# Taking all four output pieces of a feed-forward block ahead of its weight forms

## The chip, the cores and the metric

The kernel runs on one core of a Trainium2 chip. The metric is the device time of one execution in microseconds; lower is better. Its engines are named as in the profile: PE (TensorE, matrix products), DVE (VectorE), ACT (ScalarE), POOL (GpSimd) and SP (SyncE, which here issues the weight loads).

## The reference

One decoder layer on 256 tokens of width 2048, all in 32-bit floats. Two feed-forward layers stand around a token mixer (sparse attention and a gated recurrence); after each of the three a layer norm. Only the feed-forward layers matter here:

```python
def swiglu(h, w_in, w_out):
    a, b = jnp.split(h @ w_in, 2, axis=-1)
    return (jax.nn.silu(a) * b) @ w_out
...
h = layer_norm(DN_ALPHA * h + 0.5 * swiglu(h, ffn1_w_in[l], ffn1_w_out[l]), ln1_g[l], ln1_b[l])
```

`w_in` is 2048 x 11264 and `w_out` 5632 x 2048, so each layer reads 138 MB of weights.

## The kernel before

**Precision.** Every 32-bit weight and activation is split in a high half (ACT copies it to a rounded type) and a low half (DVE subtracts the high half from the original). A product takes three matmuls: high by high, high by low, low by high (`three`, lines 743 to 745).

**Blocks.** A feed-forward layer has 22 blocks (n = 0 to 21) of 256 hidden columns, `blockF` with `gate` behind it. A block's first product, tokens by `w_in`, is summed over 16 slices of 128 rows. It is done in four chunks of four slices, and in blocks 6 to 21 all four chunks use a Strassen-like scheme with 7 products of half size where 8 are usual. A chunk then has four *forms*, pieces of weights: `p1q3`, `p2`, `q5p7` and `q4p6`, with 12, 6, 12 and 12 matmuls of 256 columns. The sixteen forms of a block are called F1 to F16 here: F1 to F4 are chunk 0, F5 to F8 chunk 1, and so on; F6 is `p2` of chunk 1, F15 is `q5p7` of chunk 3. DVE makes the sums and differences of weights that a form needs (`ws` L230 for `p1q3`, L234 for `p2`, L237 for `q5p7`), then ACT (L275) and DVE (L276) split it. There is one `ws` buffer.

**Output pieces.** The second product, gate by `w_out`, is interleaved with the first as *output pieces* (`"o"` in a plan). The layer's blocks lie in segments (0-1, 2-5, 6-9, 10-13, 14-17, 18-21). While a segment's blocks are computed, the output pieces of the segment before are multiplied: four in each of the blocks 6 to 21, called O1 to O4, each 12 matmuls of 512 columns. The four add up one product of 512 output columns, which ACT then empties (`yd`, L1174) and POOL adds to a sum in memory. O1 and O3 are split like forms (`raw` L275, L276). O2 and O4 are *far* pieces: loaded and split early, with two ACT copies for each half (L182, L185) and a POOL transfer that adds the weights to the negated high half in place of DVE's subtraction.

**Order.** PE, SP and POOL run in the order in which the code emits their work. ACT and DVE are ordered by a planner when the kernel is built, which takes what is ready and, among that, what was emitted earlier. Everything is emitted piece by piece by `Weights.unit`:

```python
            self.far_to(self.cur + EARLY)
            self.load_to(self.cur + AHEAD + LOADS)
            self.split_to(self.limit or min(self.cur + AHEAD, self.cap))
            self.on_piece(self.size(self.cur) * (1 if self.pieces[self.cur][1] else 2))
```

with `EARLY = 12`, `AHEAD = 4`, `LOADS = 4`. Split weights of all pieces but the far ones go to `hl` tiles, of which there are five (`HL_BUFS`): a piece can be split when the piece five before it (far ones not counted) has been multiplied.

**Gate.** When a block's forms are done, DVE and ACT put the seven products together to `z` and multiply its two halves (L1132 to L1145). That task then lets `LAG_T[0]` pieces of the next block begin, and with the last of them, ahead of its matmuls, emits four transposes on PE (T, L1151, reading `z`, of which there is one) and the split of their result: ACT L878, DVE L879, ACT L878, DVE L879, tile `g`. With a lag of 7 T stands ahead of the block's seventh piece, which is F4 in blocks 6 to 21.

**Plans.** `block_plan(chunks, fills, lead)` puts `lead` output pieces first, then the forms, and spreads the other `fills - lead` among these. In blocks 6 to 21, with 4 fills and a lead of 3: O1 O2 O3 F1 to F8 O4 F9 to F16.

Of the kernel before, what the change touches and what calls it, by code (L numbers as in the profile page):

```python
# [22 lines left out]
SEGS = ((0, 2), (2, 6), (6, 10), (10, 14), (14, 18), (18, 22))  # L23
# [44 lines left out]
FAST = (0, 1, 2, 3)  # L68
# [4 lines left out]
def block_plan(chunks, fills, lead=2, n=4, late=True):  # L73

    plain = [("c", k) for q in range(n) if q not in chunks for k in (4 * q, 4 * q + 2)]
    forms = [(f, q) for q in chunks for f in FORMS]
    rest = ["o"] * fills
    plan = [(rest.pop(), 0) for _ in range(min(lead, fills))] + plain[:1]  # L80
    plain = plain[1:]
    slow = []
    while plain or rest:
        for which in (plain, rest) if late else (rest, plain):
            if which:
                p = which.pop(0)
                slow.append((p, 0) if p == "o" else p)
    if not forms:
        return plan + slow
    step = len(forms) / (len(slow) + 1)  # L90
    n = 0
    for i, f in enumerate(forms):
        plan.append(f)
        while len(slow) > n and i + 1 >= (n + 1) * step:
            plan.append(slow[n])
            n += 1
    return plan


FOUR = tuple(range(6, 22))  # L100


def layer_plans():
    three = (1, 2, 3)
    plans = [block_plan((), 0)] * 2
    plans += [block_plan((1, 3), 2, 0)] + [block_plan(three, 2, 2, late=False)] * 3
    for n in range(6, NBK):
        plans.append(block_plan(FAST if n in FOUR else three, 4, 3))
    return plans


FILLS = [(g, nb, 2 * p) for g, (b0, b1) in enumerate(SEGS[:-1]) for nb in range(4) for p in range(b1 - b0)]
PLANS = layer_plans()
FAST_MORE = (2, 3, 1)
AWAY = (0, 1, 4, 7, 10, 13)
# [13 lines left out]
OUT_LAST = ([(nb, k) for nb in (0, 1) for k in (0, 2, 4)] + [(nb, 6) for nb in (0, 1)]  # L129
            + [(nb, k) for nb in (2, 3) for k in (0, 2, 4, 6)])  # L130

LAG_T = (7, 6)
LAG_LN = 4
WIDE = 2
LAG_ROPE = 6
# [232 lines left out]
def tile_layer(ctx, tc, x_fm, x_tm, pos, f1a, f1o, wA, wki, wB, wG, lru, wab, wrb, wo, f2a, f2o,  # L368
# [755 lines left out]
    def ffn(x, forms, ln):  # L1124
        def gate(c, e, g, i, lag, plain):

            z = W.fast_pool.tile([P, 4 * S], F32, name=name("z"), tag="z", bufs=Z_BUFS)
            z4 = z.rearrange("p (j c) -> p j c", j=4)
            a, b = z4[:, 0:4:2], z4[:, 1:4:2]
            if e:  # L1130
                p1, p6, p7, q5 = e[0][:, :S], e[0][:, S:], e[1][:, :S], e[1][:, S:]
                A.activation(z4[:, 0], p1, AF.Copy)  # L1132
                V.tensor_tensor(z4[:, 1], z4[:, 0], p6, op=OP.add)
                V.tensor_tensor(z4[:, 2], z4[:, 1], p7, op=OP.add)
                V.tensor_tensor(b, q5[:, None, :].to_broadcast([P, 2, S]), z4[:, 1:3], op=OP.subtract)
                for t in range(2):
                    w = 512 if plain or t == 0 else S
                    zt = z[:, t * 512:t * 512 + w]
                    V.tensor_tensor(zt, zt, c[t][:, :w], op=OP.add)  # L1139
                A.activation(a, a, AF.Silu)  # L1140
            else:
                for t in range(2):
                    A.activation(z4[:, 2 * t], c[t][:, :S], AF.Silu)
                    A.activation(z4[:, 2 * t + 1], c[t][:, S:], AF.Copy)
            V.tensor_tensor(a, a, b, op=OP.mult)  # L1145
            for _ in range(lag):
                yield
            ps = BP()
            for k in range(2):
                for t in range(2):  # L1150
                    T.transpose(ps[:, k * S + t * P:k * S + (t + 1) * P], z[:, t * 512 + k * P:t * 512 + (k + 1) * P], ident)  # L1151
            with tc.high_priority() if lag == LAG_T[1] else nullcontext():
                for k in range(2):
                    hl = UHL("g")
                    split(hl, ps[:, k * S:(k + 1) * S])
                    g[i + k] = hl
# [20 lines left out]
        for s, (b0, b1) in enumerate(SEGS):  # L1177
            for n in range(b0, b1):
                c, e = blockF(x, forms, PLANS[n], fill)
                task = gate(c, e, g[s], 2 * (n - b0), LAG_T[n == NBK - 1], ("c", 0) in PLANS[n])  # L1180
                with tc.high_priority():
# [514 lines left out]
```

## Time and profile before

| | us |
|---|---|
| three runs | 2337.8, 2341.34, 2342.86 |
| median | 2341.34 |
| profiled execution | 2340.27 |
| its span, first to last instruction | 2338.4 |
| PE busy in the span | 2312.5 |
| DVE busy in the span | 2201.5 |
| ACT busy in the span | 1560.0 |

The profile is of one execution. Busy is the time in which an engine had an instruction of its own running; matmuls are pipelined and overlap, and their ends are modelled, so their starts are the better guide. An instruction that starts before the end of the one ahead of it on its engine is not an error of the table: it is how closely they follow each other.

### The profile page before, as it was taken

How to read it: one execution, taken by the hardware profiler on the slowest of the kernel's cores; microseconds unless marked ns; L12 is line 12 of the kernel's file. 1: busy time of each engine (PE TensorE's matmuls, PEld its weight loads, DVE VectorE, ACT ScalarE, POOL GpSimd, SP SyncE). 2: the span in 40 equal slices, each digit the busy share in tenths (PEclk: the TensorE clock that was granted, in tenths of full speed). 3: DMA queues.
4: the chain of work that ended last, by engine and by line, in shares of the span. 5: the costliest groups of instructions: out<-in, count | busy, mean ns of one | idle time of the engine just before them, and what ended most of it. 6: DMA issues, size and time to landing. Idle time of an engine off the chain costs nothing.

```text
span 2338.4 us, 40427 instructions
## 1 busy us (share of the span) xinstructions
PE 2312.5 (99%) x15430; PEld 2109.4 (90%) x15430; DVE 2201.5 (94%) x3196; ACT 1560.0 (67%) x2273; POOL 263.4 (11%) x368
## 2 busy tenths in 40 slices
PE   9999999999999999999999999999999999999998
PEld 7899999999988999888899998888889999999997
DVE  7999999999999999979887888998999999999997
ACT  7667777777757656556557785555667777777763
POOL 1101111111110000000100001100111111111111
PEclk9999999999999999999999999999999999999999
DMA  9878988888876556554675658655788888888875
GB/s 336 251 238 240 261 250 251 250 256 250 230 244 209 192 187 216 185 189 154 244 239 193 200 182 326 239 198 195 242 275 232 253 255 252 243 252 267 244 221 215
DMA packets 142178, 546.97 MB, mean 234 GB/s; under 512 B 16640, under 2 KB 17280, under 8 KB 117536
## 3 DMA queue, kind: packets, MB, share of 16 engines
q1 hardware_dynamic: 100800, 455.00, 55.1%
q0 software_dynamic: 41040, 89.27, 18.4%
q8 instruction: 120, 1.97, 0.3%
q14 instruction: 74, 0.61, 0.1%
q10 hardware_dynamic: 144, 0.13, 0.0%
HBM read 507.10 MB, written 37.22 MB: 233 GB/s over the span
## 4 chain that ended last, share of the span: by engine, by line
PE 66%; DVE 23%; issue 5%; DMA 3%; ACT 2%; POOL 0%; SPq 0%; ACTq 0%; DVEq 0%; POOLq 0%
PE mm L743 13%; PE mm L745 13%; PE mm L744 13%; DVE hl L276 13%; PE bp L744 5%; PE bp L745 5%; PE bp L743 4%; PE mm L1390 3%; PE mm L1389 3%; PE mm L1391 3%; DVE ws L230 2%; DVE rf L237 2%; DVE rf L234 2%; ACT hl L275 2%; DMA raw<-f1o 1%
## 5 line engine op out<-in xcount | busy, mean ns | idle before, releaser
L275 ACT ACTIVATE hl<-rf 128x1024 fp32r<-128x1024 f32 x573 | 511.3, 912 | 232.9 <-DVE rf L237 119.7
L276 DVE TENSOR_TENSOR hl<-rf,hl 128x1024 fp32r<-128x1024 f32 x573 | 596.9, 1047 | 8.2 <-ACT hl L275 3.8
L276 DVE TENSOR_TENSOR hl<-raw,hl 128x1024 fp32r<-128x1024 f32 (+3 forms) x402 | 474.2, 1196 | 62.2 <-ACT hl L275 61.4
L275 ACT ACTIVATE hl<-raw 128x1024 fp32r<-128x1024 f32 (+3 forms) x402 | 408.4, 1035 | 179.4 <-PE mm L745 82.8
L744 PE MATMUL bp<-hl,sh 128*128 128x256 f32 x1146 | 323.6, 282 | 10.1 <-DVE hl L276 10.1
L743 PE MATMUL bp<-hl,sh 128*128 128x256 f32 x1146 | 320.9, 280 | 0.0
L745 PE MATMUL bp<-hl,sl 128*128 128x256 f32 x1146 | 320.2, 279 | 0.0
L743 PE MATMUL mm<-hl,hs 128*128 128x512 f32 (+1 forms) x800 | 274.5, 343 | 1.6 <-DVE z L1139 0.7
L275 ACT ACTIVATE hl<-ws 128x1024 fp32r<-128x1024 f32 x191 | 202.0, 1058 | 102.7 <-DVE ws L230 71.5
L744 PE MATMUL mm<-hl,hs 128*128 128x512 f32 (+1 forms) x800 | 268.3, 335 | 0.0
L745 PE MATMUL mm<-hl,hs 128*128 128x512 f32 (+1 forms) x800 | 267.9, 335 | 0.1
L230 DVE TENSOR_TENSOR ws<-rf 128x1024 f32<-128x1024 f32 x191 | 233.8, 1224 | 5.4 <-DMA rf<-wrb 1.3
L276 DVE TENSOR_TENSOR hl<-ws,hl 128x1024 fp32r<-128x1024 f32 x191 | 234.2, 1226 | 1.8 <-ACT hl L275 1.7
L744 PEld LDWEIGHTS bp<-hl,sh 128*128 128x128 f32 x1146 | 215.4, 188 | 17.5 <-DVE hl L276 16.3
L745 PEld LDWEIGHTS bp<-hl,sl 128*128 128x128 f32 x1146 | 217.7, 190 | 0.0
L743 PEld LDWEIGHTS bp<-hl,sh 128*128 128x128 f32 x1146 | 215.4, 188 | 1.3
L1389 PE MATMUL mm<-hs,hl 128*128 128x256 f32 x640 | 178.3, 279 | 0.0
L1391 PE MATMUL mm<-hs,hl 128*128 128x256 f32 x640 | 177.8, 278 | 0.0
L1390 PE MATMUL mm<-hs,hl 128*128 128x256 f32 x640 | 177.7, 278 | 0.0
L743 PEld LDWEIGHTS mm<-hl,hs 128*128 128x128 f32 x800 | 150.4, 188 | 19.1 <-issue 2.6
L745 PEld LDWEIGHTS mm<-hl,hs 128*128 128x128 f32 x800 | 151.0, 189 | 16.7 <-DVE hs L937 0.5
L744 PEld LDWEIGHTS mm<-hl,hs 128*128 128x128 f32 x800 | 150.5, 188 | 14.3 <-DVE hl L276 0.2
(360 smaller groups left out, 5897.6 us busy)
## 6 DMA issues: line engine op xcount, KB each, us to landing
rf<-f1a SPq DMA_DIRECT2D x75, 1024.0 KB, 7.7
rf<-f2a SPq DMA_DIRECT2D x75, 1024.0 KB, 7.5
raw<-f1o SPq DMA_DIRECT2D x88, 512.0 KB, 6.6
raw<-f2o SPq DMA_DIRECT2D x88, 512.0 KB, 6.6
raw<-wB SPq DMA_DIRECT2D x80, 512.0 KB, 4.8
raw<-wG SPq DMA_DIRECT2D x54, 512.0 KB, 4.2
ya<-yd POOLq DMA_DIRECT2D x80, 256.0 KB, 7.4
rf<-wA SPq DMA_DIRECT2D x20, 1024.0 KB, 5.5
```

The source lines that it names most:

```text
L230: v.tensor_tensor(t, b[:, 0:4:3], b[:, 1:2].to_broadcast([P, 2, 2, 256]), op=OP.add)
L234: v.tensor_tensor(b[:, 1], t[:, 1], b[:, 0], op=OP.add)
L237: v.tensor_tensor(b[:, 0], b[:, 1], b[:, 2], op=OP.add)
L275: nc.scalar.activation(hp, src, AF.Copy)
L276: self.last = nc.vector.tensor_tensor(lp, src, hp, op=OP.subtract)
L743: T.matmul(ps, xh, w[0], start=start, stop=False)
L744: T.matmul(ps, xh, w[1], start=False, stop=False)
L745: T.matmul(ps, xl, w[0], start=False, stop=stop)
L1389: T.matmul(ps[:, :S], w[0], x[:, 0], start=first, stop=False)
L1390: T.matmul(ps[:, :S], w[0], x[:, 1], start=False, stop=False)
L1391: T.matmul(ps[:, :S], w[1], x[:, 0], start=False, stop=last)
```

## The change

Blocks that are not the first of a segment get a lead of 4: O1 O2 O3 O4 F1 to F16. The first blocks of the segments (6, 10, 14, 18) keep their plan, since their O4 multiplies the gate of the block just before. The lag of the transposes goes from 7 pieces to 5, for all blocks but the last of a layer. T then stands ahead of a block's fifth piece: between O4 and F1 in the blocks with the new plan, between F1 and F2 in blocks 6, 10, 14 and 18.

```diff
     for n in range(6, NBK):
-        plans.append(block_plan(FAST if n in FOUR else three, 4, 3))
+        plans.append(block_plan(FAST if n in FOUR else three, 4, 3 if any(n == b for b, _ in SEGS) else 4))
     return plans
...
-LAG_T = (7, 6)
+LAG_T = (5, 6)
```

## Rows read from the trace of the kernel before

**Rows 1.** The page, part 1: busy us, share of the span, instructions.
```profile
PE 2312.5 (99%) x15430; PEld 2109.4 (90%) x15430; DVE 2201.5 (94%) x3196; ACT 1560.0 (67%) x2273; POOL 263.4 (11%) x368
```
**Rows 2.** Windows, blocks 6-21 of each layer: length, busy us, clock, DMA share, GB/s.
```profile
159.30:661.61 502.31, 497.64 (x3522) 464.44 (x3521) 500.04 (x608) 361.08 (x504) 85.97 (x100) 1.00 0.85 247
1781.32:2283.43 502.11, 497.32 (x3522) 463.81 (x3521) 500.37 (x609) 360.57 (x503) 85.72 (x100) 1.00 0.83 247
```
**Rows 3.** PE's waits, whole span: total us, times, longest.
```profile
PE bp L744 <- DVE hl L276: 10.1, 30, 0.6
```
**Rows 4.** Timeline of DVE, one block: start us, us, instruction, count.
```profile
471.32 2.35 DVE L276 TENSOR_TENSOR hl<-raw,hl 128x1024 fp32r<-128x1024 f32 x2
...
480.99 0.69 DVE L1145 TENSOR_TENSOR z<-z 128x512 f32<-128x512 f32 x1
...
482.73 1.22 DVE L230 TENSOR_TENSOR ws<-rf 128x1024 f32<-128x1024 f32 x1
...
485.60 0.69 DVE L276 TENSOR_TENSOR hl<-rf,hl 128x512 fp32r<-128x512 f32 x1
...
487.94 0.42 DVE L879 TENSOR_TENSOR g<-bp,g 128x256 fp32r<-128x256 f32 x1
488.27 1.22 DVE L276 TENSOR_TENSOR hl<-rf,hl 128x1024 fp32r<-128x1024 f32 x1
489.40 0.43 DVE L879 TENSOR_TENSOR g<-bp,g 128x256 fp32r<-128x256 f32 x1
489.74 1.22 DVE L230 TENSOR_TENSOR ws<-rf 128x1024 f32<-128x1024 f32 x1
...
493.81 1.23 DVE L276 TENSOR_TENSOR hl<-ws,hl 128x1024 fp32r<-128x1024 f32 x1
495.08 1.23 DVE L230 TENSOR_TENSOR ws<-rf 128x1024 f32<-128x1024 f32 x1
...
500.30 1.22 DVE L276 TENSOR_TENSOR hl<-ws,hl 128x1024 fp32r<-128x1024 f32 x1
501.59 1.23 DVE L276 TENSOR_TENSOR hl<-rf,hl 128x1024 fp32r<-128x1024 f32 x1
502.73 2.36 DVE L276 TENSOR_TENSOR hl<-raw,hl 128x1024 fp32r<-128x1024 f32 x2
```
**Rows 5.** Timeline of PE, same block: O1, F1, F2, T, F15, F16, next O1.
```profile
472.88 0.39 PE L743 MATMUL mm<-hl,g 128*128 128x512 f32 x1
...
481.05 0.28 PE L743 MATMUL bp<-hl,xs 128*128 128x256 f32 x1
...
482.47 0.28 PE L743 MATMUL mm<-hl,xs 128*128 128x256 f32 x1
...
484.59 0.60 PE L1151 MATMUL bp<-ident,z 128*128 128x128 f32 x4
...
485.14 0.28 PE L744 MATMUL mm<-hl,xs 128*128 128x256 f32 x1
...
501.57 0.38 PE L744 MATMUL bp<-hl,sh 128*128 128x256 f32 x1 [0.39 <-DVE hl L276]
...
502.94 0.28 PE L743 MATMUL mm<-hl,xs 128*128 128x256 f32 x1
...
504.31 0.39 PE L743 MATMUL mm<-hl,g 128*128 128x512 f32 x1
```
**Rows 6.** Timeline of ACT, same block: F6's copy, gate halves, emptied product, F16's copy.
```profile
482.67 0.63 ACT L275 ACTIVATE hl<-rf 128x512 fp32r<-128x512 f32 x1 [0.35 <-PE mm L745]
...
485.23 0.38 ACT L878 ACTIVATE g<-bp 128x256 fp32r<-128x256 f32 x1
...
488.91 0.36 ACT L878 ACTIVATE g<-bp 128x256 fp32r<-128x256 f32 x1
...
495.26 1.06 ACT L1174 ACTIVATE yd<-mm 128x512 f32<-128x512 f32 x2
...
500.50 1.06 ACT L275 ACTIVATE hl<-rf 128x1024 fp32r<-128x1024 f32 x1 [1.24 <-PE mm L745]
```

## The prediction

> **What bounds the kernel now.** I read the page's busy shares first: TensorE 99%, VectorE 94% [rows 1]. A busy TensorE is no proof that it sets the pace, because its matmul ends are modelled. So I cut out the two stretches that the change touches, blocks 6 to 21 of either feed-forward layer, 16 blocks each [rows 2]. There VectorE is busy 500.04 of 502.31 us and 500.37 of 502.11 us, over 99.5%: it has as little room as TensorE, and its busy time is not modelled. A block takes 502.31 / 16 = 31.39 and 502.11 / 16 = 31.38 us. TensorE's clock is 1.00 in both.
>
> Next the waits: TensorE's largest is for VectorE's lower halves of weight forms, 30 times, at most 0.6 us [rows 3]. That is about once a block. The timeline shows which: F15, the sum form of the last chunk, whose second matmul starts at 501.57 us [rows 5], just after VectorE's subtraction that begins at 500.30 and takes 1.22 [rows 4].
>
> Then VectorE's own order. From one pair of output-piece subtractions to the next, 471.32 to 502.73, is 31.41 us [rows 4]; the reader should see in the rows between that one instruction follows another at a fixed pitch, about 1.14 us for 1024 columns, 0.60 for 512, 0.33 for 256. Two places are longer. 493.81 to 495.08 is 1.27 where 1.14 is usual: a new sum may overwrite the only buffer of sums after the old one is wholly read. 500.30 to 501.59 is 1.29: F16's subtraction waits for ScalarE's copy, which ends at 500.50 + 1.06 = 501.56 [rows 4, 6]. Together 0.28; so VectorE's instructions alone need about 31.41 - 0.28 = 31.13 us. **VectorE sets the block's time, and TensorE waits for it at F15.** None of VectorE's work is removed by the change.
>
> **The change, part by part.** No instruction is added or dropped on any engine. (1) In 12 blocks of each layer (7-9, 11-13, 15-17, 19-21), 24 in all, O4 moves from behind F8 to behind O3. Blocks 6, 10, 14 and 18 keep their order, since their O4 reads the gate of the block just before. (2) The transposes T come two pieces earlier: right behind O4 in the 24, behind F1 in those four of a layer. (3) With O4 go its weight load on SP, its ScalarE copies and two accumulating transfers on POOL, and, behind it, the two ScalarE copies that empty the product and their POOL transfers.
>
> For TensorE alone (1) and (2) look like a gain. After a run of output pieces F1's 12 matmuls take 482.47 - 481.05 = 1.42 us; F16's 12 take 504.31 - 502.94 = 1.37 [rows 5]. The quicker pace appears after an interruption such as T. With T right behind the output pieces all 168 form matmuls could have it, at most some 114 x 0.05 / 12 = 0.5 us a block. I book this at nothing: TensorE would only arrive at F15 earlier and wait longer. If VectorE were not the bound it would be worth its 0.5 us; that is a rival below.
>
> The cost I do book comes from the buffers of split weights. There are five. A form's two halves fill one; O2 and O4 use other tiles. While TensorE is on F1 to F5, F6 has to wait until F1 is done with. Today's row: ScalarE's first half of F6 starts at 482.67 after waiting 0.35 us for TensorE, 0.20 after F2 starts at 482.47 [rows 5, 6]. So there is a second loop: TensorE is let go at F15, runs F15, F16, the output pieces and F1; then F6 can be split; VectorE works from F6 to the next F15.
>
> Today's length of that loop: from F15's release (501.57) to the next block 504.31 - 501.57 = 2.74; three output pieces 481.05 - 472.88 = 8.17; F1 1.42; release to ScalarE 0.20, its copy 0.63 and 0.03 to VectorE (501.56 to 501.59) = 0.86; VectorE from F6's subtraction at 485.60 to the end of F15's at 500.30 + 1.22 = 501.52, 15.92; to TensorE 0.05. Sum 29.16, so it has 31.41 - 29.16 = 2.25 us to spare.
>
> After the change: a fourth output piece, 8.17 / 3 = +2.72. T ahead of F1: from its start at 484.59 to the second matmul behind it at 485.14 is 0.55, less one matmul pitch of 0.12, +0.43. F1 at the quick pace, -0.05. Against that, VectorE's two subtractions of the gate halves, now between F6 and F9 (487.94 to 488.27 and 489.40 to 489.74, 0.33 + 0.34) move ahead of F6: T is earlier than F1, and the code emits them behind F5 and ahead of F6. That takes out 0.67. But the one at 487.94 filled the time in which ScalarE copied F8; without it I put the 0.13 of the other chunk there. 29.16 + 2.72 + 0.43 - 0.05 - 0.67 + 0.13 = **31.72 us**, 0.31 over the 31.41 now. VectorE's own loop would be 31.41 + 0.13 = 31.54, so the buffer loop ends last.
>
> Bounds of that 0.31: the two uncovered spots of 0.13 inside the loop may both be filled, giving 31.46; or both gate subtractions may stay inside it and cover one of them, 31.72 + 0.67 - 0.13 = 32.26. The gate's way is two-legged: its second half on ScalarE (488.91) starts only after VectorE's first at 487.94 is done [rows 4, 6]. First copy 0.64 after T (485.23 against 484.59), VectorE, second copy, VectorE: some 2.0 us where F6 is ready 1.8 + 0.86 us after T's start. It just fits, so I take the value without it.
>
> In the six blocks 10, 14 and 18 of the two layers T behind F1 leaves F8 uncovered, 6 x 0.13 = 0.8 us; blocks 6 start with VectorE ahead, none. Blocks 1 to 5 get T two pieces sooner; nothing waits for it there, 0.
>
> The moved side work I cost at nothing. The product's copies, two in 1.06 us at 495.26 [rows 6], now fall between T and F6's copy on ScalarE, in about 1.8 us that also holds 0.38 of the gate: full, not over. If that cover is gone, F6 slips and the price is at most 0.5 us a block. T needs z, ready at 480.99 + 0.69 = 481.68 [rows 4] against 484.59 now; T moves less than 1 us earlier against F15's release, so it doesn't wait. SP's later loads stand behind O4's, whose buffers were freed a block before.
>
> Sum: 24 x 0.31 = 7.4, + 0.8 = 8.2 us. The profiled execution took 2340.27 us (span 2338.4), 1.07 under the median of the runs; it would become 2348.5, and on the median's scale 2341.34 + 8.2 = **2349.5 us**.
>
> **Rivals.** *Nothing changes (0.27).* VectorE's own loop stays the longer one: the planner that orders VectorE and ScalarE is run anew, and fills the two spots of 0.13. Then a block takes 31.41 to 31.54, and 24 blocks add 0 to 3.1, with the 0.8 0 to 4 us: 2341 to 2345. For it: the difference, 0.31, is only 1% of a loop made of many rows. Against: F7 and F8 wait for F2 and F3 just as F6 waits for F1, so reordering alone hardly shortens it.
>
> *Faster (0.08).* TensorE is the bound after all, and its quicker pace counts: 24 x 0.5 = 12 us, 2329; or, with VectorE still at its limit but all its waits gone, 24 x 0.28 = 6.7, 2335. It decides from the point where VectorE needs less than TensorE's 4 x 2.72 + 0.43 + 168 x 1.37 / 12 = 30.5 us a block. Against: its instructions alone take 31.13.
>
> *Slower still (0.11).* The gate's subtractions fall behind F6: 32.26, 24 x 0.85 + 0.8 = 21 us, 2362.5; with one of them, 0.33 - 0.13 more than the forecast, 2354. For it: that is where the planner puts them now. Against: they are emitted ahead of F6 now.
>
> *Each stretch at its own bound (0.01).* If no work were carried over between output pieces and forms, a block would take 4 x 2.72 for the pieces on TensorE and 4 x (489.74 - 482.73 - 0.67) = 25.4 for the forms on VectorE [rows 4, 5], 36.2 us, and the kernel 24 x 4.8 = 115 us more, 2457. Against: five buffers carry a whole chunk over, and VectorE is busy through the output pieces too [rows 4]. The Trainium skill, Perfetto Trace Analysis, "Optimization Strategy", says that where the most contended engine changes over time, interleaving the regimes may help; by that rule the change goes the wrong way, and the rows agree in sign while leaving most of that price out.
>
> **How the numbers follow.** Forecast 0.53. A measurement of this kernel tells about 0.2% (4.7 us) from no change. Slower by more: 0.53 + 0.11 + 0.01 = 0.65; within: 0.27; faster: 0.08. The range leaves out the faster case and the last few per cent above both gate halves' price: 2339 to 2361. Within the forecast alone, 31.62 to 31.9 a block, it would be 2347 to 2354.
>
> **What would show it.** Right: in a changed block ScalarE's copy of F6 waits for TensorE longer than 0.35 us, VectorE idles before F6's, F7's or F8's subtraction, its period rises to about 31.7, form matmuls all run at the quick pace, and TensorE waits over 1 us a block at F13 to F15. Wrong: the period stays at 31.4 with no such wait (no change), or VectorE's gate rows stand between F6 and F9 (slower still). I would be wrong in kind if TensorE had no waits left and the block fell under 31.1.

## The result and the profile after

The changed kernel takes 2365.05 us (median of 4 runs, 2362.67 to 2366.02), the one before 2342.1 on the same chip: a ratio of 1.0101, interval 1.0085 to 1.0117. It is slower by 23 us, where the forecast said 8.2, and 20 at the upper end of its range. The profiled execution took 2364.12 us.

First, the page's busy line of the changed kernel, which answers to [rows 1], and the windows over blocks 6 to 21 of both layers, which answer to [rows 2]:

```profile
PE 2323.3 (98%) x15430; PEld 2112.8 (89%) x15430; DVE 2208.2 (93%) x3196; ACT 1562.1 (66%) x2273; POOL 261.7 (11%) x368
```
```profile
159.59:675.78 516.19, 504.59 (x3523) 468.80 (x3521) 504.47 (x609) 362.75 (x505) 85.08 (x100) 0.99 0.80 244
1794.91:2307.51 512.60, 501.48 (x3522) 464.34 (x3521) 504.42 (x609) 362.14 (x505) 85.14 (x100) 1.00 0.80 246
541.87:545.51 3.64, 3.64 (x20) 3.64 (x19) 3.57 (x6) 1.74 (x3) 0.00 (x0) 0.53 1.02 341
```

The stretches grew by 13.9 and 10.5 us [rows 2], all of the loss; VectorE, idle for under 2.3 us in either before, is now idle for 11.7 and 8.2. (The third row is of one spot, below.) The waits of the whole span answer to [rows 3]. The last row, ScalarE's wait for a load of the first layer, was 0.5 us in two waits before; in the second layer's stretch it is now 4.5 us in three, before none:

```profile
PE mm L744 <- DVE hl L276: 12.5, 25, 0.9
PE bp L744 <- DVE hl L276: 8.8, 23, 0.5
PE mm L743 <- ACT hl L275: 8.0, 5, 5.5
ACT wd L182 <- DMA raw<-f1o: 7.0, 3, 2.5
```

**An ordinary changed block.** Timelines of one block with the new plan: TensorE, then VectorE, then ScalarE, as in [rows 4 to 6].

```profile
479.65 0.39 PE L744 MATMUL bp<-hl,sh 128*128 128x256 f32 x1 [0.39 <-DVE hl L276]
...
482.38 0.39 PE L743 MATMUL mm<-hl,g 128*128 128x512 f32 x1
...
493.28 0.60 PE L1151 MATMUL bp<-ident,z 128*128 128x128 f32 x4
493.64 0.37 PE L743 MATMUL bp<-hl,xs 128*128 128x256 f32 x1
...
495.10 0.28 PE L743 MATMUL mm<-hl,xs 128*128 128x256 f32 x1
...
507.58 0.39 PE L744 MATMUL mm<-hl,xs 128*128 128x256 f32 x1 [0.65 <-DVE hl L276]
...
511.66 0.39 PE L744 MATMUL bp<-hl,sh 128*128 128x256 f32 x1 [0.38 <-DVE hl L276]
```
```profile
480.81 2.35 DVE L276 TENSOR_TENSOR hl<-raw,hl 128x1024 fp32r<-128x1024 f32 x2
...
494.49 0.41 DVE L879 TENSOR_TENSOR g<-bp,g 128x256 fp32r<-128x256 f32 x1
494.82 0.68 DVE L234 TENSOR_TENSOR rf<-ws,rf 128x512 f32<-128x512 f32 x1
495.42 0.41 DVE L879 TENSOR_TENSOR g<-bp,g 128x256 fp32r<-128x256 f32 x1
495.96 0.69 DVE L276 TENSOR_TENSOR hl<-rf,hl 128x512 fp32r<-128x512 f32 x1
496.57 0.68 DVE L237 TENSOR_TENSOR rf<-rf 128x512 f32<-128x512 f32 x1
497.44 1.23 DVE L276 TENSOR_TENSOR hl<-ws,hl 128x1024 fp32r<-128x1024 f32 x1 [0.18 <-ACT hl L275]
...
510.38 1.22 DVE L276 TENSOR_TENSOR hl<-ws,hl 128x1024 fp32r<-128x1024 f32 x1
511.68 1.23 DVE L276 TENSOR_TENSOR hl<-rf,hl 128x1024 fp32r<-128x1024 f32 x1
512.82 2.35 DVE L276 TENSOR_TENSOR hl<-raw,hl 128x1024 fp32r<-128x1024 f32 x2
```
```profile
494.94 0.39 ACT L878 ACTIVATE g<-bp 128x256 fp32r<-128x256 f32 x1 [0.58 <-DVE g L879]
495.30 0.63 ACT L275 ACTIVATE hl<-rf 128x512 fp32r<-128x512 f32 x1
495.84 0.62 ACT L182 ACTIVATE wd<-raw 128x512 fp32r<-128x512 f32 x1
496.36 1.05 ACT L275 ACTIVATE hl<-ws 128x1024 fp32r<-128x1024 f32 x1
```

The block takes 512.82 - 480.81 = 32.01 us, not 31.41. The loop of buffers can be read off: F15's release at 479.65, O1 at 482.38, T at 493.28, F2 at 495.10 (F1 is done with), F6's copy at 495.30, F6's subtraction at 495.96, F15's at 510.38, the next release at 511.66. Both gate subtractions (494.49 and 495.42) stand ahead of F6's. And a far copy of ScalarE (495.84) stands between F6's and F7's copies: F7's ends at 496.36 + 1.05 = 497.41, and VectorE, through with the row before by about 497.17, waits for it until 497.44.

**The last changed block of a segment** (9, 13, 17). ScalarE, then TensorE:

```profile
533.45 1.05 ACT L275 ACTIVATE hl<-ws 128x1024 fp32r<-128x1024 f32 x1
536.72 1.15 ACT L182 ACTIVATE wd<-raw 128x512 fp32r<-128x512 f32 x2 [2.22 <-DMA raw<-f1o]
537.77 1.14 ACT L185 ACTIVATE wd<-raw 128x512 fp32r<-128x512 f32 x2
538.82 2.51 ACT L275 ACTIVATE hl<-rf 128x1024 fp32r<-128x1024 f32 x3
```
```profile
539.91 0.40 PE L743 MATMUL mm<-hl,xs 128*128 128x256 f32 x1 [0.60 <-ACT hl L275]
...
541.17 0.39 PE L744 MATMUL mm<-hl,xs 128*128 128x256 f32 x1 [0.87 <-DVE hl L276]
```

ScalarE waits 2.22 us for the load of a far piece, the O4 of the block after this one, with F12's copy queued behind; then TensorE waits 0.60 and 0.87, and from 541.87 its granted clock is 0.53 for 3.64 us (the third window above), about the lower of its two levels, 1.2 GHz in place of 2.4. Such a block takes 33.6 to 33.9 us in the first layer, and 32.8 to 32.9 in the second, where the clock stays up.

The load itself takes longer than it did. Its issue, and that of POOL's transfers of the emptied product (`ya`), in the changed kernel and then in the kernel before:

```profile
525.66 0.74 SPq L175 DMA_DIRECT2D raw<-f1o  x1
525.69 1.77 POOL L1175 DMA_DIRECT2D ya<-yd  x2 [20.79 <-ACT yd L1174]
```
```profile
496.13 1.77 POOL L1175 DMA_DIRECT2D ya<-yd  x2 [4.30 <-ACT yd L1174]
515.59 0.63 SPq L175 DMA_DIRECT2D raw<-f1o  x1
```

In both kernels the load is issued 3.2 to 3.5 us after the gate's last multiplication (L1145). ScalarE gets to its copy 8.6 to 8.9 us after the issue in the changed kernel and 8.3 to 8.6 before, so no sooner. But the six loads of this kind land 10.1 to 11.3 us after their issue, and 7.2 to 8.8 before. The product's transfers, which moved with O4, are now issued within 1 us of each of the six, and were issued 18 us or more ahead before.

### The profile page after: what moved, and what is told of

The parts are those of the page before. It is cut to its first block, busy times and chain, and to the rows that moved or that the text cites. A ratio compares the mean times of both kernels' runs of the same rounds, so it can differ in the third digit from the quotient of the medians.

```text
span 2362.3 us, 40329 instructions
## 1 busy us (share of the span) xinstructions
PE 2323.3 (98%) x15430; PEld 2112.8 (89%) x15430; DVE 2208.2 (93%) x3196; ACT 1562.1 (66%) x2273; POOL 261.7 (11%) x368
## 4 chain that ended last, share of the span: by engine, by line
PE 59%; DVE 28%; issue 5%; ACT 5%; DMA 3%; SPq 0%; POOL 0%; ACTq 0%; DVEq 0%; POOLq 0%
DVE hl L276 15%; PE mm L744 13%; PE mm L745 13%; PE mm L743 12%; DVE ws L230 5%; PE bp L744 4%; PE bp L745 4%; PE bp L743 3%; ACT hl L275 3%; PE mm L1389 3%; PE mm L1391 3%; PE mm L1390 3%; DVE rf L237 2%; DVE rf L234 2%; DMA raw<-f2o 1%
## 5 line engine op out<-in xcount | busy, mean ns | idle before, releaser
L275 ACT ACTIVATE hl<-rf 128x1024 fp32r<-128x1024 f32 x573 | 508.8, 910 | 197.7 <-PE mm L745 104.9
L276 DVE TENSOR_TENSOR hl<-rf,hl 128x1024 fp32r<-128x1024 f32 x573 | 590.4, 1040 | 18.8 <-ACT hl L275 13.2
```

The source lines that it names most:

```text
L275: nc.scalar.activation(hp, src, AF.Copy)
L276: self.last = nc.vector.tensor_tensor(lp, src, hp, op=OP.subtract)
```

## The experiments

Beside each median and ratio stand the sums of blocks 6 to 21 of either layer, gate to gate (from one start of L1132 to another), from the profiled execution, and the rest of its span (all us). Each ratio is to the kernel before on the same chip, where its own median was 2339.8 to 2342.1. In the kernels with far copies behind, lines have numbers that are one or two higher.

| kernel | median | ratio to before | layer 1 | layer 2 | rest |
|---|---|---|---|---|---|
| before | 2341 | 1 | 503.0 | 502.9 | 1332.5 |
| changed | 2365.05 | 1.0101 | 516.8 | 513.0 | 1332.5 |
| lag alone | 2349.39 | 1.0039 (1.0024 to 1.0054) | 508.2 | 505.9 | 1333.5 |
| order alone | 2355.0 | 1.007 (1.0055 to 1.0085) | 511.9 | 509.7 | 1331.1 |
| changed, late far copies behind | 2355.22 | 1.007 (1.0055 to 1.0085) | 511.0 | 510.7 | 1333.9 |
| changed, all far copies behind | 2354.0 | 1.0063 (1.0046 to 1.008) | 510.4 | 510.6 | 1331.3 |
| the same, five buffers, 49 of U | 2351.9 | 1.0048 (1.0033 to 1.0063) | 508.9 | 508.8 | 1333.1 |
| the same, six buffers, 49 of U | 2347.51 | 1.0031 (1.002 to 1.0041) | 503.5 | 503.8 | 1335.9 |
| changed, six buffers only | 2359.6 | 1.0079 (1.0064 to 1.0094) | 511.7 | 509.1 | 1339.5 |
| before, far copies behind | 2341.26 | 1.0004 (0.9994 to 1.0013) | 502.9 | 503.2 | 1333.8 |
| the same, lag of 5 | 2341.78 | 1.0001 (0.9992 to 1.001) | 503.1 | 503.1 | 1333.4 |
| before, behind, six buffers, 49 of U | 2348.8 | 1.0036 (1.0023 to 1.0049) | 502.6 | 502.6 | 1344.7 |

### One half of the change alone

```diff
-LAG_T = (7, 6)
+LAG_T = (5, 6)
```

> The kernel before with the lag of 5 alone; the plans keep three output pieces, forms, the fourth. Buffer-loop theory (F6's split waits until F1 is multiplied, and the fourth output piece ahead of F1 takes the room out of that loop): T behind F1 costs 0.43 us of the 2.25 that the loop had to spare, so VectorE's period stays 31.4 and the time is within 0.2% of the kernel before, 2338 to 2346. Rival, that the earlier transposes and gate halves are the cost: most of the 23 us come back, 2355 to 2365.

Missed. The lag alone costs 0.39%. Most blocks keep 31.45 us, but ScalarE waits for a load five times in the first layer, 3.9 us in all, and four times in the second, 1.8 us. The longest wait:

```profile
496.43 1.16 ACT L182 ACTIVATE wd<-raw 128x512 fp32r<-128x512 f32 x2 [2.41 <-DMA raw<-f1o]
```

So late loads come without the new order too, by another way: where neither kernel waits, the far copy comes 8.22 us after its load's issue, and 8.55 before. The other half, the changed kernel with the lag put back to 7:

> The changed plans with the old lag of 7: O1 to O4, F1, F2, T. Buffer-loop theory: T's 0.43 us leaves the way to F6, but both gate halves (0.67 us on VectorE) come to stand between F6 and F9, inside the loop, covering one wait of 0.13: a period of about 31.7 + 0.27 (far copy ahead of F7) - 0.43 + 0.67 - 0.13 = 32.1 us in an ordinary changed block, and the late loads at the segments' ends stay: 2362 to 2370, as the change. Rival, that the earlier T is the cost: 2340 to 2348.

It costs 0.7%, and 2355.0 us lies 7 under the expected range: the late loads stay, landing 10.1 to 11.1 us after their issue, but ScalarE waits 5.9 us for them in all, not 11.5, and the clock is 1.00 in both stretches. Ordinary changed blocks take 31.9 to 32.1 us with T two pieces later, as expected, though not by the terms of that sum: in the block that was read no far copy stands ahead of F7's, and VectorE waits 0.35 us for F7's copy all the same. The long block is the order's, not the transposes'.

### Far copies ordered behind the forms' copies

```diff
-            for c in range(2):
+            with self.behind(k):
...
+    W.behind = lambda k: tc.issue_after(W.copy.ins)
```

The last line is that of the second run. The first does it for the far pieces alone whose load came late, the O4 of the first block of a segment:

> The change, with the ScalarE copies of one far piece a segment (O4 of blocks 6, 10, 14, 18, whose load is issued late in the block ahead) ordered behind the newest form's copy, so that ScalarE doesn't wait for that load with forms queued behind it. In-order ScalarE theory: the waits for raw of 7.0 and 4.5 us, three in each layer, go, and with them the three stretches at half clock: 8 to 13 us less than the change, 2352 to 2357; ordinary changed blocks keep 32.0. Rival, that memory traffic as such is late there and something else waits next: under 3 us gained.

No ScalarE row waits for such a load any more, no stretch is at half clock, and the changed kernel's sums fall by 516.8 + 513.0 - 511.0 - 510.7 = 8.1 us. Ordinary changed blocks stay at 32.0 to 32.1. Then for all far pieces:

> The same for all far pieces: F7's copy also loses the far copy of 0.52 us that the planner put in front of it. In-order ScalarE theory: VectorE's wait before F7's subtraction falls from 0.26 to near 0, ordinary changed blocks from 32.02 to about 31.75, so some 18 x 0.27 = 5 us less than the run with the late ones alone: 2347 to 2352, still above the kernel before by the 0.31 a block of the buffer loop. Rival, that F7 waits for its buffer and not for ScalarE's order: no difference to the run with the late ones alone.

Missed: a further 0.7 us in the sums, no more. F7's wait is gone, but four far copies (498.09 to 500.17 us) now stand ahead of F12's copy. TensorE waits there instead:

```profile
502.98 0.38 PE L746 MATMUL mm<-hl,xs 128*128 128x256 f32 x1 [1.24 <-DVE hl L277]
```

Controls, in the order of before. With all far copies behind:

> The kernel before with all far copies ordered behind the forms' copies on ScalarE, nothing else. Buffer-loop theory: before has 2.25 us to spare in that loop, so it costs nothing and gains nothing: 2336 to 2345, a period of 31.4. Rival (the ordering of far copies itself costs what is left in the changed kernel with it, some 0.6 us a block): 2350 to 2356.

and with a lag of 5 as well:

> The plan of before (O1 O2 O3 F1 to F8 O4), the transposes two pieces earlier (lag 5), and all far copies ordered behind the forms' copies on ScalarE. The lag alone cost 0.39%, with late raw loads in front of the forms' copies. Theory that this cost is the late loads alone: it goes, 2338 to 2346 us, and a block takes 31.4 to 31.5. Rival (the earlier transposes themselves lengthen a block): 2347 to 2353.

Neither can be told from the kernel before. So the lag's 0.39% hung on where the far copies stand on ScalarE (8.2 us in the sums, of which 5.7 are seen as waits for loads), and the edit itself costs nothing.

### Six buffers of split weights

To the changed kernel with all far copies behind (U is the pool of 128x512 tiles from which the far pieces' split halves come; it gives up four tiles as room for the sixth buffer):

```diff
-U_BUFS = 53
+U_BUFS = 49
...
-HL_BUFS = 5
+HL_BUFS = 6
```

> The changed kernel with all far copies ordered behind the forms' (as in the run before this), with six buffers of split weights in place of five, and 49 buffers of U in place of 53 to make room. Buffer-loop theory: with six buffers F7, not F6, is the first form that has to wait until F1 is multiplied. VectorE can do F6's subtraction ahead of the transposes, so about one form's work (some 1.1 us) leaves the loop: it falls from 32.05 to about 31.0 us, under VectorE's own 31.4 to 31.5. A block then takes 31.4 to 31.5, the 24 changed blocks lose their 0.6, and the time falls by about 14 us, to 2338 to 2346. Rival (the order of copies on ScalarE, or TensorE's order itself, makes the block long, whatever the number of buffers): 2351 to 2357, as with five.

> Control: the same kernel with five buffers of split weights and 49 of U. Buffer-loop theory: 2352 to 2357, the same as with 53 buffers of U, so that what six buffers give is theirs. Rival (fewer U buffers move the loads by themselves): it moves by more than 3 us from 2354.0.

With five buffers, VectorE (gate subtraction, F6's, F15's, and the first row of this block and of the next) and ScalarE's copy of F6:

```profile
475.04 2.35 DVE L277 TENSOR_TENSOR hl<-raw,hl 128x1024 fp32r<-128x1024 f32 x2
...
489.66 0.41 DVE L881 TENSOR_TENSOR g<-bp,g 128x256 fp32r<-128x256 f32 x1
490.18 0.69 DVE L277 TENSOR_TENSOR hl<-rf,hl 128x512 fp32r<-128x512 f32 x1
...
504.39 1.22 DVE L277 TENSOR_TENSOR hl<-ws,hl 128x1024 fp32r<-128x1024 f32 x1
...
506.82 1.22 DVE L277 TENSOR_TENSOR hl<-raw,hl 128x1024 fp32r<-128x1024 f32 x1
```
```profile
489.52 0.63 ACT L276 ACTIVATE hl<-rf 128x512 fp32r<-128x512 f32 x1
```

With six, the same spots; the three copies from 480.09 include F6's:

```profile
471.43 2.35 DVE L277 TENSOR_TENSOR hl<-raw,hl 128x1024 fp32r<-128x1024 f32 x2
...
486.04 0.42 DVE L881 TENSOR_TENSOR g<-bp,g 128x256 fp32r<-128x256 f32 x1
486.38 0.68 DVE L277 TENSOR_TENSOR hl<-rf,hl 128x512 fp32r<-128x512 f32 x1
...
503.02 2.36 DVE L277 TENSOR_TENSOR hl<-raw,hl 128x1024 fp32r<-128x1024 f32 x2
```
```profile
480.09 2.53 ACT L276 ACTIVATE hl<-rf 128x1024 fp32r<-128x1024 f32 x3
483.42 1.28 ACT L1176 ACTIVATE yd<-mm 128x512 f32<-128x512 f32 x2 [0.80 <-PE mm L747]
```

With five, F6's copy comes after T and the gate, and VectorE stands still before F6 (490.18 - 489.66 = 0.52 where 0.33 is usual). With six it is done before the product is emptied, and F6's subtraction follows the gate's at the usual 0.34. The block goes from 31.78 to 31.59, others from 31.96 to the same, and the two sums from 1017.7 to 1007.3: 10.4 us less, 1.4 above before. Some 3.5 of the 10.4 stand in block 7 of either layer alone, which takes 30.1 to 30.3 us; blocks 14 to 17 fall from 127.1 us to 126.15, where the kernel before has 125.6 to 125.8. The median fell by 4.4 alone, to 1.5 above the time expected: the rest of the span grew, by 2.8 in the profiled execution, which was the quickest of eight. That is a price elsewhere, as the control in the order of before shows:

> Control: the kernel before with far copies behind, six buffers of split weights and 49 of U. Buffer-loop theory: the loop has room with five already in this order, so a sixth buffer gives nothing: 2337 to 2346, a block at 31.4. Rival (a sixth buffer helps any order, so that what it gave the changed kernel says nothing of this loop): faster by 4 us or more, 2330 to 2337.

Missed by 2.8 us, but not the rival's way. The sums move by -0.9 us from the kernel with five, with single blocks of the first half between 30.9 and 31.9, and the rest of the span grows by 10.9: six buffers give the stretches nothing where the loop is short. The 10.9 belong to six buffers and 49 of U together, as no run in this order has 49 of U and five. (In the changed order 49 of U in place of 53 took 2.1 us off the median by themselves, on another chip, and 3.3 off the sums.)

The Trainium skill, Perfetto Trace Analysis, "Optimization Strategy", says that a gap which repeats for a stretch of the kernel on the engine that should be saturated can mean too few buffers. By that rule a sixth should close VectorE's gap ahead of F6; the trace agrees: the pitch there falls from 0.52 to 0.34.

With six buffers, and the far copies left where the planner puts them:

> The changed kernel with six buffers of split weights and 49 of U, its far copies left where the planner puts them. Buffer-loop theory with late loads as a second, separate cost: the blocks that wait for no load take 31.5 to 31.6, as in the run with six buffers and far copies behind; what is left is the late loads', some 8 us: 2350 to 2357. Rival (a sixth buffer covers late loads as well): 2343 to 2349.

It falls 2.6 us above what was expected, and rather than 31.5 to 31.6 most of its ordinary blocks take 31.74 to 31.88, three in the first segments 31.53 to 31.66. Those that wait for loads take 32.5 to 34.4. In an ordinary one, ScalarE and then VectorE:

```profile
589.68 1.14 ACT L182 ACTIVATE wd<-raw 128x512 fp32r<-128x512 f32 x2
590.72 1.99 ACT L275 ACTIVATE hl<-rf 128x1024 fp32r<-128x1024 f32 x2
```
```profile
591.79 1.23 DVE L276 TENSOR_TENSOR hl<-rf,hl 128x1024 fp32r<-128x1024 f32 x1 [0.34 <-ACT hl L275]
```

Two far copies ahead of F8's copy: here the wait for ScalarE is seen with no lack of buffers.

### Far copies by GpSimd

```diff
-                nc.scalar.activation(l[c], t[:, c * 512:(c + 1) * 512], AF.Copy, scale=-1.0)
+                nc.gpsimd.tensor_scalar(l[c], t[:, c * 512:(c + 1) * 512], -1.0, None, OP.mult)
...
-                nc.scalar.activation(h[c], t[:, c * 512:(c + 1) * 512], AF.Copy)
+                nc.gpsimd.tensor_copy(h[c], t[:, c * 512:(c + 1) * 512])
```

> The changed kernel with the far pieces' copies made by GpSimd in place of ScalarE; nothing is left out. It takes every far copy, late or not, out of the forms' way on ScalarE. Theory that the far copy ahead of F7's copy is what made the buffer loop longer than forecast (31.72 + 0.27): an ordinary changed block takes 31.7 to 31.8, no block waits for a load, and the time is 2343 to 2352. Rival (the loop's excess over the forecast is elsewhere, as in the run with all far copies behind): 31.9 to 32.1 a block, 2352 to 2357. Rival (GpSimd's copies slow VectorE's subtractions or are too long themselves): VectorE's 1.14 us per 1024 columns rises, slower than 2357.

> Control: the same copies by GpSimd in the order of before. Theory: ScalarE's far copies cost nothing there, 2337 to 2346, a block at 31.4. Rival (GpSimd slows VectorE): the same addition as in the changed kernel, over 2346.

2471.53 us (ratio 1.0563, 1.0547 to 1.0579) in the changed kernel and 2502.4 (1.0692, 1.0676 to 1.0708) in that of before: the last rival, in both. In the changed order, groups of 140 us of the first layer:

```profile
L182 POOL TENSOR_SCALAR wd<-raw 128x512 fp32r<-128x512 f32 x17 | 42.9, 2524 | 11.2 <-DMA raw<-f1o 11.2
```
```profile
L276 DVE TENSOR_TENSOR hl<-rf,hl 128x1024 fp32r<-128x1024 f32 x33 | 44.8, 1368 | 0.4
```

A GpSimd row of L182 takes 2.52 us on average (spans on GpSimd are rough) where ScalarE's takes 0.62, and VectorE's subtraction of 1024 columns lasts 1368 ns, 1223 in the same stretch before. VectorE's slowdown hides what the edit was to show, so this experiment says nothing of the far copies.

### Less work for VectorE

In the order of before with far copies behind, O3 becomes a far piece, which takes one subtraction of 1024 columns a block off VectorE:

```diff
-                if k in (2, 6) and (g or nb >= 2):
+                if k in (2, 4, 6) and (g or nb >= 2):
```

> The same as v2_before_far_behind, and O3 too is loaded and split as a far piece, which takes one subtraction of 1024 columns (1.14 us) a block away from VectorE and gives ScalarE and POOL's transfers its work. Theory that VectorE sets the block's time before the change: a block falls to VectorE's 31.41 - 1.14 = 30.3 us or to TensorE's 30.9, 0.5 to 1.1 us less in 32 blocks, and the time is 2305 to 2326. Rival (TensorE already is as close to its bound): 2336 to 2345; or the far transfers come too late or collide with the loads (90% of the transfer engines' time is a ceiling seen nowhere in these stretches): slower than 2345.

> The order of before with far copies behind, O3 far too (1.14 us a block off VectorE), and the transposes two pieces earlier. With the late transposes that gave 31.35 us a block, TensorE's matmuls of the forms at the slower pace for most of the block. Theory that TensorE now sets the block and that earlier transposes bring its quicker pace two forms sooner: 2 x 12 x 0.005 = 0.1 us a block, 2338 to 2343. Rival (what VectorE lost in work does not come through, for another wait of 0.4 us): unchanged, 2341 to 2345. Either way no version of this kind is faster than before by over 0.2%.

The first takes 2343.05 us (1.0009, 1.0 to 1.0018): no gain, the rival. Its sums are 501.3 and 501.4, 3.2 us under before, but most of that is the last block's, whose gate starts some 2.3 us sooner in either layer; blocks 14 to 17 take 125.6 us, and 125.6 to 125.8 before. TensorE's waits for VectorE in the first stretch fall only from 4.7 us to 2.9. The second, with the lag of 5, takes 2337.15 (0.9985, 0.9976 to 0.9995), its sums are 498.7 and 498.4: 0.17 us a block under the first, where 0.1 was expected. Blocks 14 to 17 take 124.8 us, 0.2 a block under before. It is the one version here that beats both kernels, if by under 0.2%; its 2337.15 us lies 0.85 under the expected range. In the changed order with six buffers:

> The changed order with six buffers, far copies behind, and O3 too as a far piece, which takes 1.14 us a block from VectorE. With the order of before, that moved the bound to TensorE, at 31.35 us a block, much of it at the slower of its two paces (0.118 us between matmuls of 256 columns). Theory that transposes right behind the output pieces keep TensorE at the quicker pace (0.113): 4 x 2.72 + 0.35 + 168 x 0.1135 = 30.3 us, at most 0.9 us less in each of 24 blocks, 2315 to 2333. Rival (the slower pace comes back in every other block, as in the run with six buffers): 30.6 to 31.2, 2328 to 2342. Rival (the transfers, whose engines were busy 94% with the order of before, come late): slower than 2342.

It takes 2470.53 us (1.0549, 1.0524 to 1.0574), the last rival. TensorE waits for the transfers that make the far pieces' lower halves:

```profile
PE mm L746 <- DMA wd<-f1o: 40.0, 17, 5.2
PE mm L746 <- DMA wd<-f2o: 35.6, 17, 4.7
```

## Why the prediction was wrong

**What bounds the kernel.** "VectorE sets the block's time" was half of it. With 1.14 us a block taken off VectorE the repeating blocks lost next to nothing (125.6 us for four, as before), with earlier transposes 0.2 each: TensorE, at its two paces, needed hardly less time than VectorE. That the loss would not be hidden holds either way.

**The buffer loop** was right in mechanism, and nearly so in size. Term by term, the ordinary block above against the forecast: release to O1 2.73 (2.74); O1 to T 10.90 (8.17 + 2.72); T to F2 1.82 (0.43 + 1.37); to F6's copy 0.20 (0.20); to F6's subtraction 0.66 (0.66); from there to the end of F15's, 511.60 - 495.96 = 15.64 (15.92 - 0.67 + 0.13 = 15.38); to TensorE some 0.05. All but one are on the forecast, the gate subtractions moved ahead of F6 as said, and T ahead of F1 met no wait for z. With the far copies behind, five buffers and 49 of U, the shortest changed blocks took 31.77 to 31.80, where the forecast was 31.72; the one shown has 505.61 - 490.18 = 15.43 for its last long term, and the others take up to 32.0, with more spots of 0.12 to 0.16 uncovered on VectorE. Six buffers take the loop away and leave 31.55 to 31.6: VectorE's own loop, forecast at 31.54. So the rival that nothing changes falls, and so does the reading of an order on TensorE that costs by itself.

**The step that failed** is "The moved side work I cost at nothing." Of that work, the product's copies on ScalarE did fit. The far copies and their loads didn't, in two ways.

First, in front of a form's copy: the 15.64 is 0.26 over its forecast, and F7's subtraction waited about 0.26 for a copy behind a far copy, in 22 of the 24 changed blocks: 6 us by the rows, which no run took away alone. "If that cover is gone … at most 0.5 us a block" held this price, but I named F6 as what would slip, and it was F7. Putting far copies behind at one place moved them ahead of F12 instead: ScalarE was under 71% busy in these stretches, but in the block read its idle spots between T and F12's copy were 0.53 us or shorter, and a far piece's four copies take 2.1.

Second, late loads, which I didn't price at all. ScalarE works in the planner's order, and a far copy whose load isn't in holds up every form's copy behind it. Before, there was no slack: the far copy at 492.73 us starts 0.02 after its load lands, without a wait. The lag alone brings such copies 0.3 us sooner after their loads' issue. The order alone makes six loads land some 2 to 3 us later, beside the product's transfers that moved with O4; ScalarE then gets to their copies 9.6 to 9.8 us after the issue, and with both halves of the change 8.6 to 8.9. That these transfers lengthen the loads is read from the trace; no run took them away. The late loads cost 8.1 us here, by the run that orders their copies behind, part of it through the half clock in three blocks of the first layer. I had taken that "SP's later loads stand behind O4's, whose buffers were freed a block before" settles loads. It speaks of when their buffers come free, not of how long the loads take, nor of when the copy that needs them is put in the queue.

**The sum.** The stretches grew by 1029.8 - 1005.9 = 23.9 us. Late loads: 8.1. The other 15.8 are 0.66 a changed block: by the rows the forecast's 0.31, some 0.26 for F7, and 0.09 for the rest, such as the second block of a segment in the first layer, 32.41 rather than 32.01, which I didn't follow further. The 0.8 for blocks 10, 14 and 18 did not come (31.40). The runs show the loop's share, but not this split: with late loads gone and F7 free the excess is still 1021.0 - 1005.9 = 15.1, as TensorE waits at F12 instead. With 49 of U it is 1017.7 - 1005.9 = 11.8, 0.49 a changed block, and six buffers take 10.4 of it.

**The rivals.** "Slower still", 2362.5, comes close to the measured time by luck: the gate subtractions did not fall behind F6. TensorE's quicker pace is seen (in the block above in over 150 of 168 form matmuls, in the one before it in under 50) and is worth nothing, as booked: in the block above it waits 0.65 at F12 and 0.38 at F15 instead. The price of each stretch at its own bound, 4.8 us a block, was far off. That case's rule of the Trainium skill, Perfetto Trace Analysis, "Optimization Strategy" (interleaving regimes may help), has the sign that the runs show, at 0.5 to 0.7 us a block without the late loads.

## What to carry to other kernels

When work moves in an in-order queue, list what stands in that queue next to it, and ask of each entry whether its input has slack: a copy that starts as its load lands can block everything behind it after a small shift, and a transfer that moves beside that load can be the shift. A loop through a pool of buffers can be summed from a timeline, here to 0.1 to 0.3 us a block, and one more buffer tests it, but the control must show what that buffer costs elsewhere. Taking work from an engine that is 99% busy gives only as much as the next engine leaves: measure that before counting on it.

## What was not expected

- Waits of TensorE of 0.60 and 0.87 us, between 539.31 and 541.17, were followed from 541.87 by 3.64 us at a granted clock of 0.53, with matmuls 0.213 us apart for 0.113. This happened in three blocks of the first layer and in none of the second.
- A sixth buffer of split weights, with 49 of U, lengthened the rest of the span by 10.9 us in the order of before; in the changed order with far copies behind it did so by about 3 against 49 of U and five. What there costs it stays open.
- TensorE's matmuls of 256 columns go at 0.118 or 0.113 us. With T right behind O4 all blocks could have gone at the quicker pace; in the run with six buffers one block did for the most part, and the next went at 0.118 from F1 to F15. What sets the pace stays open.
